# The gate and up products of a decoder layer's FFN by one Strassen step

## The chip, the cores and the metric

One NeuronCore of a Trainium2 chip runs the whole kernel. The metric is the device time of one execution in microseconds (us). TensorE (PE in the profile) multiplies, VectorE (DVE), ScalarE (ACT) and GpSimd (POOL) do the elementwise work, and SyncE (SP), ScalarE and GpSimd issue the transfers. The inputs and the output are float32.

## The reference

One decoder layer on 512 tokens of width 1024: an input projection, sixteen attention heads, a state-space branch, two gated projections that are merged into `w_out`, a layer norm, and a gated feed-forward network (FFN) of hidden width 2816 with a second layer norm. The change lies in the last part:

```
x = layer_norm(DEEPNORM_ALPHA * x + mixed, ln1_g, ln1_b)
h = (silu(x @ w_ffn_gate) * (x @ w_ffn_up)) @ w_ffn_down
x = layer_norm(DEEPNORM_ALPHA * x + h, ln2_g, ln2_b)
```

`x` is 512 by 1024, the gate and up weights are 1024 by 2816, the down weights 2816 by 1024.

## The kernel before

**Products in three parts.** Every float32 operand is split into a high part (a cast to float32r on ScalarE, line 65) and a low part (source minus high part, on VectorE, line 66). A product is three matmuls, high by high, high by low, low by high (`mm3`, lines 97 to 100). Each matmul contracts 128 rows, and each has its own weight load (PEld).

**Weights.** `load_w` (line 85) fetches 128 x 1024 float32 (512 KB) on SP's queue into one of 4 `raw` buffers and splits it into one of 3 `whi` and 3 `wlo` buffers. The split is marked as high priority. The scheduler of the Tile framework writes a fixed order of instructions for each engine from the program order and these priorities, and each engine keeps to its order.

**The output projection, `w_out`** (lines 629 to 692). Its 8 weight chunks come in two halves of 512 columns. Six are loaded and split ahead, the last two of half 0 during the second pair of token tiles (`wo_chunk`, line 638). Tokens go in two rounds `th_` of two tiles of 128: matmuls, `evac_res` (lines 668 to 671, residual and statistics), `layer_norm` (lines 673 to 683), then `transpose_in` (line 165) turns each tile by eight PE transposes and splits it into `x1T`.

**FFN gate and up** (`ffn_pair`, line 709). The hidden width goes in 11 pairs of 128 columns. For each pair the gate product is accumulated over 8 blocks of 128 in PSUM (`gps` banks), then the up product (`cps` banks). Tokens are 512 matmul columns wide, except in the first pair, which does tokens 0 to 255 first and then 256 to 511, so that it can start before the second round is normed. ScalarE takes the tanh of the gate (line 715), VectorE multiplies (lines 716 and 719), and the product `h` is split at once into 22 pairs of 128 x 512 tiles.

**FFN down** (`gemm_down`, line 135) takes the 22 blocks of `h` as stationary operand in two halves of 512 output columns; the last 4 chunks of the second half (`tail`) are done tile by tile of tokens, so that each tile is normed and stored while the next is multiplied.

Of the kernel before, what the change touches and what calls it, by code (L numbers as in the profile page):

```python
# [9 lines left out]
F32 = mybir.dt.float32  # L10
F32R = mybir.dt.float32r
# [26 lines left out]
def tile_hybrid_decoder_layer(  # L38
# [32 lines left out]
    def cps():  # L71
# [13 lines left out]
    def load_w(src, a, b, dst=None):  # L85

        raw = stream.tile([P, 1024], F32, name="raw", bufs=4)
        nc.sync.dma_start(out=raw.rearrange("p (a b) -> p a b", a=a), in_=src.rearrange("(a p) c -> p a c", p=P))
        if dst is None:
            dst = ([stream.tile([P, 1024], F32R, name="whi")], [stream.tile([P, 1024], F32R, name="wlo")])  # L90
# [6 lines left out]
    def mm3(o, l, r, start, stop):  # L97
        nc.tensor.matmul(out=o, lhsT=l[0], rhs=r[0], start=start, stop=False)  # L98
        nc.tensor.matmul(out=o, lhsT=l[0], rhs=r[1], start=False, stop=False)  # L99
        nc.tensor.matmul(out=o, lhsT=l[1], rhs=r[0], start=False, stop=stop)  # L100

# [210 lines left out]
    def group_u(g, ys, gz):  # L312
        uh, ul = big("uh", 4, F32R), big("ul", 4, F32R)
        for c in range(NT):
            cs = slice(c * P, (c + 1) * P)
            y = ys[c]
            nc.vector.scalar_tensor_tensor(out=y, in0=y, scalar=0.5, in1=gz[:, c, :], op0=ALU.mult, op1=ALU.mult)
            ss = sb.tile([P, 2], F32, name="ss")
# [61 lines left out]
    def att_head(h, qk, vt, of):  # L380
# [4 lines left out]
        for i in range(NT):  # L385
            n = (i + 1) * P
            qs = slice(i * P, (i + 1) * P)
            ps = cps()
            nc.tensor.matmul(out=ps[:, 0:n], lhsT=q1[:, qs], rhs=k1[:, 0:n], start=True, stop=False)  # L389
            nc.tensor.matmul(out=ps[:, 0:n], lhsT=q2[:, qs], rhs=k2[:, 0:n], start=False, stop=True)  # L390
            sm = sb.tile([P, 3], F32, name="sm", bufs=6)
# [60 lines left out]

    wraw = stream.tile([P, 1024], F32, name="raw", bufs=4).rearrange("p (a b) -> p a b", a=KD)
    nc.gpsimd.memset(wraw, 0.0)
# [33 lines left out]

    wfh = stream.tile([P, 1024], F32R, name="whi").rearrange("p (a b) -> p a b", a=KD)
    wfl = stream.tile([P, 1024], F32R, name="wlo").rearrange("p (a b) -> p a b", a=KD)  # L490
    split(wfh, wfl, wraw)
# [146 lines left out]
    def wo_chunk(kc, half, dst=None):  # L638
        if (kc, half) not in wo:
            wo[(kc, half)] = down_chunk(w_o, kc, half)  # L640
        return wo[(kc, half)]

    for pair in range(4):
        def evac_a(b, ps):
# [10 lines left out]
    def load_gb(gv, bv):  # L655
        t = slot("gz", (P, 2, D))
# [9 lines left out]
    st6 = [sb.tile([P, 2, 6], F32, name=f"st6{tt}", bufs=1) for tt in range(NT)]  # L666

# [5 lines left out]
    def layer_norm(tt, gb, parts=1):  # L673
        mv = sb.tile([P, 4], F32, name="mv", bufs=4)
        nc.vector.bn_aggr(out=mv[:, 0:2], in_=st6[tt])
# [21 lines left out]
    hslots = []  # L697
    for tag in ("xtok", "xtok", "uh", "ul"):
        b_ = big(tag, 4, F32R)
        hslots += [b_[:, i, :] for i in range(4)]  # L700
    for tag in QK[0] + QK[1] + ("y", "y", "hn"):
        hslots += [slot(tag, (P, T), F32R) for _ in range(2)]
    hT = [(hslots[2 * i], hslots[2 * i + 1]) for i in range(NH - 3)]
    FT = ("dx", "yo", "xw", "sq")

    def ffn_chunks(j2, dst=None):
        return [[ws_chunk(w, j2 * 256, half, dst if w is w_fu and half == 1 else None) for half in range(2)] for w in (w_fg, w_fu)]

    def ffn_pair(j2, s_, chunks=(None, None)):
        n = s_.stop - s_.start  # L710
        t = {}

        def evac_fg(b, ps):
            t[b] = slot(FT[b + 2 * (j2 % 2)])[:, 0:n]
            nc.scalar.activation(out=t[b], in_=ps, func=AF.Tanh, scale=0.5)
            nc.vector.scalar_tensor_tensor(out=t[b], in0=t[b], scalar=1.0, in1=ps, op0=ALU.add, op1=ALU.mult)

        def evac_fu(b, ps):
            nc.vector.scalar_tensor_tensor(out=t[b], in0=t[b], scalar=0.5, in1=ps, op0=ALU.mult, op1=ALU.mult)
            hi, lo = hT[2 * j2 + b]  # L720
            split(hi[:, s_], lo[:, s_], t[b])
        gemm_ws(w_fg, j2 * 256, KD, lambda kt: cols(x1T, kt, s_), evac_fg, gps, n, chunks[0])
        gemm_ws(w_fu, j2 * 256, KD, lambda kt: cols(x1T, kt, s_), evac_fu, cps, n, chunks[1])

    t = [slot("ab", (P, T), F32R) for _ in range(4)]
    chunks = ffn_chunks(0, (t[0:2], t[2:4]))
    ffn_pair(0, slice(0, 256), chunks)
    ffn_pair(0, slice(256, T), chunks)
    hT += [(slot("ab", (P, T), F32R), slot("ab", (P, T), F32R)) for i in range(3)]
    for j2 in range(1, NH // 2):  # L730
        ffn_pair(j2, slice(0, T))

    gb = load_gb(ln2_g, ln2_b)

# [13 lines left out]
    t = [slot(tag, (P, T), F32R) for tag in FT]  # L748
# [31 lines left out]
```

## Time and profile before

| | us |
|---|---|
| three runs | 1166.93, 1169.84, 1170.02 |
| median | 1169.84 |
| profiled execution, its own time | 1168.29 |
| its span, first to last instruction | 1166.6 |
| PE busy in the span | 1140.0 (98%) |
| VectorE busy | 680.6 (58%) |
| ScalarE busy | 468.9 (40%) |
| GpSimd busy | 102.8 (9%) |

The profile shows one execution. A matmul's shown duration includes its way through the array, so the rate is read from the distance between starts. A row "from <- releaser" names the instruction whose end let an idle engine go on. Times are in us from the span's start.

### The profile page before, as it was taken

To read this page: it belongs to the slowest core of one execution; us is meant where nothing else is said; L and a number is where in the kernel's file an instruction comes from. 1 tells how busy PE (TensorE), PEld (TensorE's weight loads), DVE (VectorE), ACT (ScalarE), POOL (GpSimd) and SP (SyncE) were. 2 spreads that over 40 slices of the span, in tenths; PEclk is the share of its full clock that TensorE was granted. 3 is DMA by queue.
4 is the path that set the end of the run, shared out by engine and by line. 5 is a ranking of instruction groups with operands and counts; after the bars stand their busy time and mean duration, and the time that the engine had idled before them with its cause. 6 is when DMAs were issued, how large, how long until landed. Compare 5 with 4: busy or idle time off the path is not lost.

```text
span 1166.6 us, 14040 instructions
## 1 busy us (share of the span) xinstructions
PE 1140.0 (98%) x5390; PEld 926.4 (79%) x5390; DVE 680.6 (58%) x1118; ACT 468.9 (40%) x834; POOL 102.8 (9%) x137
## 2 busy tenths in 40 slices
PE   6999999999999999999999999999999999999997
PEld 5887877778777788777777888889888888888885
DVE  3579964883885664897788345555433433432326
ACT  3376763453441423665566353202323223222120
POOL 2003131030231100210110000010000000000001
PEclk8999999999999999999999999999999999999999
DMA  7343242233221233121212355601333233232221
GB/s 237 98 130 126 74 127 90 77 115 98 91 92 56 89 92 107 39 72 55 73 55 56 91 163 161 196 21 56 107 97 102 91 104 95 91 107 92 91 72 72
DMA packets 93427, 112.58 MB, mean 97 GB/s; under 512 B 4820, under 2 KB 72624, under 8 KB 93232
## 3 DMA queue, kind: packets, MB, share of 16 engines
q1 hardware_dynamic: 90880, 107.03, 29.6%
q10 hardware_dynamic: 1152, 4.19, 1.1%
q0 software_dynamic: 1328, 0.46, 0.3%
q8 instruction: 42, 0.69, 0.2%
q14 instruction: 25, 0.20, 0.1%
HBM read 109.38 MB, written 2.16 MB: 96 GB/s over the span
## 4 chain that ended last, share of the span: by engine, by line
PE 51%; DVE 2%; ACT 0%; issue 0%; POOL 0%; DVEq 0%; ACTq 0%
PE gps L100 11%; PE gps L98 11%; PE gps L99 11%; PE cps L98 5%; PE cps L100 5%; PE cps L99 5%; PE cps L411 1%; PE cps L417 1%; DVE t_sd L682 0%; PE cps L389 0%; PE cps L390 0%; DVE t_sd L670 0%; DVE st L671 0%; PE cps L171 0%; POOL mv L677 0%
## 5 line engine op out<-in xcount | busy, mean ns | idle before, releaser
L66 DVE TENSOR_TENSOR wlo<-raw,whi 128x1024 fp32r<-128x1024 f32 x171 | 210.1, 1229 | 336.7 <-ACT whi L65 336.4
L65 ACT CAST whi<-raw 128x1024 fp32r<-128x1024 f32 x171 | 179.8, 1051 | 418.8 <-PE gps L99 133.5
L98 PE MATMUL gps<-xh,whi 128*128 128x512 f32 (+1 forms) x648 | 252.4, 390 | 0.0
L99 PE MATMUL gps<-xl,whi 128*128 128x512 f32 (+1 forms) x648 | 252.4, 389 | 0.0
L100 PE MATMUL gps<-xh,wlo 128*128 128x512 f32 (+1 forms) x648 | 252.2, 389 | 0.0
L98 PEld LDWEIGHTS gps<-xh,whi 128*128 128x128 f32 x648 | 122.1, 188 | 22.6 <-issue 0.2
L99 PEld LDWEIGHTS gps<-xl,whi 128*128 128x128 f32 x648 | 122.2, 189 | 22.4 <-issue 0.2
L100 PEld LDWEIGHTS gps<-xh,wlo 128*128 128x128 f32 x648 | 122.1, 188 | 21.6
L98 PE MATMUL gps<-whi,xh 128*128 128x512 f32 x208 | 82.7, 398 | 4.4 <-ACT xh L65 4.4
L100 PE MATMUL gps<-whi,xl 128*128 128x512 f32 x208 | 82.4, 396 | 0.0
L99 PE MATMUL gps<-wlo,xh 128*128 128x512 f32 x208 | 82.3, 396 | 0.0
L98 PE MATMUL cps<-xh,whi 128*128 128x512 f32 (+1 forms) x176 | 66.9, 380 | 0.0
L100 PE MATMUL cps<-xh,wlo 128*128 128x512 f32 (+1 forms) x176 | 66.8, 379 | 0.0
L99 PE MATMUL cps<-xl,whi 128*128 128x512 f32 (+1 forms) x176 | 66.8, 379 | 0.0
L677 POOL TENSOR_TENSOR mv<-mv,neghalf 128x1 f32<-128x1 f32 x8 | 9.5, 1192 | 558.6 <-DVE mv L676 558.6
L196 DVE SCALAR_TENSOR_TENSOR t_v<-gps,cw,t_v 128x511 f32<-128x511 f32 (+2 forms) x72 | 53.5, 745 | 3.9 <-ACT t_v L193 3.1
L100 PE MATMUL gps<-t_uh,wlo 128*128 128x512 f32 x128 | 51.0, 399 | 0.0
L99 PE MATMUL gps<-t_ul,whi 128*128 128x512 f32 x128 | 51.0, 398 | 0.0
L98 PE MATMUL gps<-t_uh,whi 128*128 128x512 f32 x128 | 50.5, 395 | 0.0
L98 PEld LDWEIGHTS gps<-whi,xh 128*128 128x128 f32 x208 | 39.7, 191 | 13.6 <-ACT xh L65 5.0
L99 PEld LDWEIGHTS gps<-wlo,xh 128*128 128x128 f32 x208 | 39.7, 191 | 8.6 <-DVE wlo L66 0.5
L100 PEld LDWEIGHTS gps<-whi,xl 128*128 128x128 f32 x208 | 39.6, 190 | 8.4 <-DVE xl L66 0.3
(548 smaller groups left out, 1913.1 us busy)
## 6 DMA issues: line engine op xcount, KB each, us to landing
raw<-in_w_in_dram SPq DMA_DIRECT2D x80, 512.0 KB, 3.7
raw<-in_w_ffn_gate_dram SPq DMA_DIRECT2D x22, 512.0 KB, 3.6
raw<-in_w_ffn_up_dram SPq DMA_DIRECT2D x22, 512.0 KB, 3.6
raw<-in_w_ffn_down_dram SPq DMA_DIRECT2D x22, 512.0 KB, 3.5
t_ab<-ac_d SPq DMA_DIRECT2D x32, 256.0 KB, 3.3
raw<-in_w_proj_ssm_dram SPq DMA_DIRECT2D x16, 512.0 KB, 3.4
raw<-in_w_out_dram SPq DMA_DIRECT2D x8, 512.0 KB, 4.0
raw<-in_w_proj_attn_dram SPq DMA_DIRECT2D x8, 512.0 KB, 4.1
```

The costliest lines, as they stand in the source:

```text
L65: nc.scalar.copy(out=hi, in_=src)
L66: nc.vector.tensor_tensor(out=lo, in0=src, in1=hi.bitcast(F32), op=ALU.subtract)
L98: nc.tensor.matmul(out=o, lhsT=l[0], rhs=r[0], start=start, stop=False)
L99: nc.tensor.matmul(out=o, lhsT=l[0], rhs=r[1], start=False, stop=False)
L100: nc.tensor.matmul(out=o, lhsT=l[1], rhs=r[0], start=False, stop=stop)
L196: nc.vector.scalar_tensor_tensor(out=v[:, sh:], in0=ps[:, 0:T - sh], scalar=cw[:, k, blk:blk + 1], in1=v[:, sh:], op0=ALU.mult, op1=ALU.add)
L411: nc.tensor.transpose(out=ps[:, o:o + P], in_=pr[i][:, kb * P:(kb + 1) * P], identity=ident)
L417: nc.tensor.matmul(out=po[:, kb * P:], lhsT=vt[:, kb, hh, :], rhs=pT[kb][j], start=kb == 0 and j == 0, stop=kb == NT - 1 and j == 1)
L677: nc.gpsimd.tensor_tensor(out=mv[:, 2:3], in0=mv[:, 2:3], in1=neghalf[:, 0:1], op=ALU.pow)
```

## The change

The hidden width goes in 5 blocks of 512 and one of 256. A block's gate product, and its up product, is a 2 by 2 by 2 problem: the block's columns, the 512 tokens and the 1024 contracted rows are each halved. Instead of eight products of quarters there are seven, on sums and differences of quarters, each with 256 tokens as matmul columns.

**Token operands.** Seven operands: two plain quarters (B11, B21) of tokens 0 to 255, split when the first round of tokens is turned; five others (NT1, NT2, T3, T4, B22), made by VectorE (`x_operands`) from a float32 copy `xf` of both rounds, once, and split. All blocks use them.

**Weight operands.** For each gemm seven fetches: a11, a12, a22 plain; s1 and s3 are each a plain fetch on SP's queue and a second, accumulating transfer on GpSimd's queue. VectorE makes the other two sums. All seven are split (`op`, high priority) into four rotating pairs of buffers (`wop0`, `wop1`).

**Sums of products.** Passes with the same bank X, Y or Z accumulate there; ScalarE copies three intermediate states to SBUF (`keep`), VectorE adds (`add`), and the four quadrants then go through the same tanh and multiplications as before.

**Other edits.** `h` is kept in float32 and split at the start of the down phase. The normed tokens go to DRAM on GpSimd's queue and come back for the second residual on ScalarE's queue. All 8 `w_out` chunks are split ahead; the last two follow the attention projection. The last stage's `tail` is 3 chunks and not 4. Buffers are in pools on two sides of SBUF, and a tile waits only for the older tiles under it.

```diff
+    for kc in range(2, 4):
+        t = [slot(tag, (P, T), F32R) for tag in QK[kc - 2]]
+        wo[(kc, 0)] = down_chunk(w_o, kc, 0, (t[0:2], t[2:4]))
...
         for tt in tts:
             for _ in layer_norm(tt, gb):
                 pass
-            transpose_in(x1T, xr[tt], tt)
+            nc.gpsimd.dma_start(out=x1_d[tt], in_=xr[tt])
+            for i in range(2):
+                ps = cps()
+                for k in range(4):
+                    kt = 4 * i + k
+                    nc.tensor.transpose(out=ps[:, k * P:(k + 1) * P], in_=xr[tt][:, kt * P:(kt + 1) * P], identity=ident)
+                ps = ps.rearrange("p (k t) -> p k t", k=4)
+                ts = slice(tt * P, (tt + 1) * P)
+                if th_ == 0:
+                    hi, lo = xop[("B11", "B21")[i]]
+                    split(hi[:, :, ts], lo[:, :, ts], ps)
+                nc.scalar.copy(out=xf[i][:, :, ts], in_=ps)
...
+        nt1 = t_tile().rearrange("p (k t) -> p k t", k=4)
+        v.tensor_tensor(out=nt1, in0=B[1, 1], in1=B[1, 2], op=ALU.subtract)
+        nt2 = new("NT2", lambda t: v.scalar_tensor_tensor(out=t, in0=nt1, scalar=-1.0, in1=B[2, 2], op0=ALU.mult, op1=ALU.subtract))
+        xop["NT1"] = operand(top, "nt1")
+        split(*xop["NT1"], nt1)
+        new("T3", lambda t: v.tensor_tensor(out=t, in0=B[2, 2], in1=B[1, 2], op=ALU.subtract))
+        xop["B22"] = operand(top, "b22")
+        split(*xop["B22"], B[2, 2])
+        new("T4", lambda t: v.scalar_tensor_tensor(out=t, in0=nt2, scalar=-1.0, in1=B[2, 1], op0=ALU.mult, op1=ALU.subtract))
...
+        def load(*src):
+            t = tile_()
+            nc.sync.dma_start(out=v(t), in_=src[0])
+            for s_ in src[1:]:
+                nc.gpsimd.dma_start(out=v(t), in_=s_, accum_op=ALU.add)
+            return t
+
+        def op(t):
+            p_ = wops[nops[0] // 2 % 2]
+            nops[0] += 1
+            o = [p_.tile([P, 1024], F32R, name="w" + i, bufs=2)[:, 0:4 * F] for i in "hl"]
+            with tc.high_priority():
+                split(*o, t)
+            return [v(i) for i in o]
+
+        a11, a12 = load(q(1, 1)), load(q(1, 2))
+        s1 = load(q(2, 1), q(2, 2))
+        s3 = load(q(2, 1), q(1, 1))
+        a22 = load(q(2, 2))
+        yield op(a11)
+        yield op(a12)
+        with tc.high_priority():
+            nc.vector.tensor_tensor(out=a11, in0=s1, in1=a11, op=ALU.add)
+        yield op(a11)
+        yield op(s1)
+        yield op(s3)
+        with tc.high_priority():
+            nc.vector.tensor_tensor(out=a12, in0=a11, in1=a12, op=ALU.add)
+        yield op(a12)
+        yield op(a22)
+
+    PASSES = (("X", "B11"), ("Y", "B21"), ("X", "NT2"), ("Z", "NT1"), ("X", "T3"), ("Z", "B22"), ("X", "T4"))
...
+        for i, (b, x_) in enumerate(PASSES):
...
+            hi, lo = next(ops)
+            xo = xop[x_]
+            for j in range(nj):
+                js = slice(j * P, (j + 1) * P)
+                for k in range(4):
+                    mm3(ps[:, j * 256:(j + 1) * 256], (hi[:, k, js], lo[:, k, js]), (xo[0][:, k, :], xo[1][:, k, :]),
+                        first and j == 0 and k == 0, j == nj - 1 and k == 3, True)
+            if i == 0:
+                keep("a", ps)
+            elif i == 1:
+                quadrant(0, 0, add("a", ps), 1.0)
+            elif i == 2:
+                keep("b", ps)
+            elif i == 3:
+                keep("d", ps)
+            elif i == 4:
+                quadrant(1, 1, add("d", ps), -1.0)
+            elif i == 5:
+                quadrant(0, 1, add("b", ps), 1.0)
+            else:
+                quadrant(1, 0, ps, -1.0)
+            yield
...
+    for b in range(6):
+        gate, up = ffn_block(b)
+        if b == 0:
+            for gen in (gate, up):
+                for _ in range(2):
+                    next(gen)
+            x_operands()
+        for gen in (gate, up):
+            for _ in gen:
+                pass
...
+    for k2 in range(2):
+        h_split(0, k2, t_tile(F32R), t_tile(F32R))
...
+    for b in range(1, 6):
+        for k2 in range(2 if b < 5 else 1):
+            h_split(b, k2, *[htp.tile([P, 1024], F32R, name=f"ht{b}{k2}{i}") for i in "hl"])
...
-    gemm_down(wd_chunk, NH, lhs_h, range(NT), 1, evac_last, lambda: banks.pop(0), 4, (t[0:2], t[2:4]))
+    gemm_down(wd_chunk, NH, lhs_h, range(NT), 1, evac_last, lambda: banks.pop(0), 3)
```

## Rows read from the trace of the kernel before

**Rows 1.** The page: busy time by engine, and the chain that ended last, by engine
```profile
PE 1140.0 (98%) x5390; PEld 926.4 (79%) x5390; DVE 680.6 (58%) x1118; ACT 468.9 (40%) x834; POOL 102.8 (9%) x137
...
PE 51%; DVE 2%; ACT 0%; issue 0%; POOL 0%; DVEq 0%; ACTq 0%
```

**Rows 2.** Timeline of PE, 512-column matmuls: first and last of 57 (start, duration)
```profile
779.84 0.40 PE L99 MATMUL gps<-wlo,xh 128*128 128x512 f32 x1
...
792.55 0.39 PE L98 MATMUL gps<-t_ul,xh 128*128 128x512 f32 x1
```

**Rows 3.** Timeline of PE, 256-column matmuls: first and last of 57
```profile
811.74 0.28 PE L98 MATMUL gps<-xh,whi 128*128 128x256 f32 x1
...
818.46 0.28 PE L100 MATMUL cps<-xh,wlo 128*128 128x256 f32 x1
```

**Rows 4.** Timeline of PE: first 512-column matmul of gate, first of down
```profile
821.46 0.40 PE L98 MATMUL gps<-xh,whi 128*128 128x512 f32 x1
...
1039.09 0.39 PE L98 MATMUL cps<-whi,t_xtok 128*128 128x512 f32 x1
```

**Rows 5.** The chain after the output projection (start, us, what)
```profile
793.85 0.24 PE gps L100
794.11 0.70 DVE t_sd L670
...
796.16 1.20 DVE xl L66 x2
...
800.62 1.29 DVE t_sd L682
...
802.05 1.06 PE cps L171 x8
803.15 1.09 PE cps L171 x8
```

**Rows 6.** VectorE by line, 849 to 1029 (count, busy us, mean ns, idle before)
```profile
L66 DVE TENSOR_TENSOR wlo<-raw,whi 128x1024 fp32r<-128x1024 f32 x33 | 40.4, 1225 | 81.3 <-ACT whi L65 81.3
L716 DVE SCALAR_TENSOR_TENSOR t_dx<-t_dx,gps 128x512 f32<-128x512 f32 x5 | 3.4, 688 | 6.1 <-ACT t_dx L715 6.1
```

**Rows 7.** ScalarE by line, 849 to 1029
```profile
L65 ACT CAST whi<-raw 128x1024 fp32r<-128x1024 f32 x34 | 35.8, 1053 | 92.6 <-PE cps L99 40.3 <-issue 34.8 <-PE gps L99 17.5
L715 ACT ACTIVATE t_dx<-gps 128x512 f32<-128x512 f32 x5 | 3.0, 598 | 9.2 <-PE gps L100 9.2
```

**Rows 8.** Stretches: length; PE, PEld, DVE, ACT, POOL busy (instructions); clock, DMA, GB/s
```profile
849.00:1029.00 180.00, 180.00 (x796) 149.10 (x795) 72.77 (x82) 53.69 (x67) 0.00 (x0) 1.00 0.31 97
1039.00:1099.00 60.00, 60.00 (x267) 49.69 (x266) 17.75 (x18) 12.12 (x12) 0.00 (x0) 1.00 0.29 97
```

**Rows 9.** Timeline of PE at the kernel's start, after a wait of 3.42 us
```profile
15.55 0.80 PE L98 MATMUL gps<-whi,xh 128*128 128x512 f32 x1 [3.42 <-ACT xh L65]
...
19.13 0.63 PE L100 MATMUL gps<-whi,xl 128*128 128x512 f32 x1
19.56 0.63 PE L98 MATMUL gps<-whi,xh 128*128 128x512 f32 x1
...
21.66 0.48 PE L98 MATMUL gps<-whi,xh 128*128 128x512 f32 x1
```

**Rows 10.** DMA issues (count, KB each, median us from issue to landing)
```profile
raw<-in_w_ffn_gate_dram SPq DMA_DIRECT2D x22, 512.0 KB, 3.6
...
raw<-in_w_in_dram POOLq DMA_DIRECT2D x1, 128.0 KB, 6.7
```

**Rows 11.** Timeline of GpSimd: issue of the transfer of 128 KB
```profile
9.41 0.93 POOL L455 DMA_DIRECT2D raw<-in_w_in_dram  x1
```

**Rows 12.** Timeline of VectorE, the last but one tile of tokens
```profile
1153.65 0.69 DVE L670 SCALAR_TENSOR_TENSOR t_sd<-t_sd,gps 128x512 f32<-128x512 f32 x1 [0.99 <-PE gps L100]
...
1156.74 1.41 DVE L682 SCALAR_TENSOR_TENSOR t_sd<-t_sd,mv,t_gz 128x512 f32<-128x512 f32 x2
```

**Rows 13.** Timeline of VectorE: last low part made for the output projection
```profile
753.50 0.69 DVE L651 SCALAR_TENSOR_TENSOR xl<-t_y,xh 128x512 fp32r<-128x512 f32 x1
```

More of the change, by code (lines that the diff above doesn't have):

```diff
@@ L665, in tile_hybrid_decoder_layer @@
         xr.append(t)
-    st6 = [sb.tile([P, 2, 6], F32, name=f"st6{tt}", bufs=1) for tt in range(NT)]
+    st6 = [cst0.tile([P, 2, 6], F32, name=f"st6{tt}") for tt in range(NT)]
     def evac_res(half, tt, ps):
@@ L673, in layer_norm @@
     def layer_norm(tt, gb, parts=1):
-        mv = sb.tile([P, 4], F32, name="mv", bufs=4)
+        mv = cst0.tile([P, 4], F32, name="mv", bufs=4)
         nc.vector.bn_aggr(out=mv[:, 0:2], in_=st6[tt])
@@ L683, in layer_norm, with h_tile, operand @@
             yield s_
-    gb = load_gb(ln1_g, ln1_b)
-    x1T = new_act()
+    gb = load_gb(slot("gz", (P, 2, D)), ln1_g, ln1_b)
+    x1_d = dram.tile([NT, P, D], F32, name="x1_d")
+    right1.close()
+    right2, left2 = ExitStack(), ExitStack()
+    ha = pool(ctx, "ha", "right")
+    bop = pool(right2, "bop", "right")
+    rqp = pool(right2, "rqp", "right")
+    wops = [pool(right2, "wop0", "right")]
+    def h_tile(b):
+        return (hb if b < 4 else ha).tile([P, 4 * T], F32, name="h" if b < 4 else "xf", bufs=4 if b < 4 else 2)
+    xf = [h_tile(4).rearrange("p (k t) -> p k t", k=4) for _ in range(2)]
+    def operand(p_, nm):
+        return [p_.tile([P, 4, 256], F32R, name=nm + i) for i in "hl"]
+    xop = {"B11": operand(bop, "b11"), "B21": operand(bop, "b21")}
     for th_ in range(2):
@@ L693, in tile_hybrid_decoder_layer @@
                 pass
-            transpose_in(x1T, xr[tt], tt)
[L697 to L723, printed above, removed]
@@ new lines, in tile_hybrid_decoder_layer, with t_tile, x_operands, new @@
+    left1.close()
+    hb = pool(ctx, "hb", "left")
+    tp = pool(ctx, "tp", "left")
+    top = pool(left2, "top", "left")
+    wops.append(pool(left2, "wop1", "left"))
+    nops = [0]
+    tmp2 = pool(left2, "tmp2", "left")
+    def t_tile(dtype=F32):
+        return tp.tile([P, 1024], dtype, name="T", bufs=4)
+    def x_operands():
+        B = {(k, t): xf[k - 1][:, :, (t - 1) * 256:t * 256] for k in (1, 2) for t in (1, 2)}
+        def new(nm, make):
+            t = t_tile().rearrange("p (k t) -> p k t", k=4)
+            make(t)
+            xop[nm] = operand(top, nm.lower())
+            split(*xop[nm], t)
+            return t
+        v = nc.vector
+        nt1 = t_tile().rearrange("p (k t) -> p k t", k=4)
[7 more added lines that the diff above has]
+        new("T4", lambda t: v.scalar_tensor_tensor(out=t, in0=nt2, scalar=-1.0, in1=B[2, 1], op0=ALU.mult, op1=ALU.subtract))
@@ new lines, in tile_hybrid_decoder_layer, with ffn_gemm, keep, add @@
+    PASSES = (("X", "B11"), ("Y", "B21"), ("X", "NT2"), ("Z", "NT1"), ("X", "T3"), ("Z", "B22"), ("X", "T4"))
+    def ffn_gemm(w, c0, F, alloc, quadrant):
+        nj = F // P
+        n = nj * 256
+        ops = quarters(w, c0, F)
+        bank = {}
+        cp = {}
+        def keep(nm, src):
+            cp[nm] = tmp2.tile([P, T], F32, name="cp", bufs=4)[:, 0:n]
+            nc.scalar.copy(out=cp[nm], in_=src)
+        def add(nm, src):
+            nc.vector.tensor_tensor(out=cp[nm], in0=src, in1=cp[nm], op=ALU.add)
+            return cp[nm]
+        for i, (b, x_) in enumerate(PASSES):
+            first = b not in bank
+            if first:
+                bank[b] = alloc()[:, 0:n]
+            ps = bank[b]
+            hi, lo = next(ops)
[20 more added lines that the diff above has]
+            yield
@@ new lines, in tile_hybrid_decoder_layer, with ffn_block, gate, up @@
+    hs = []
+    def ffn_block(b):
+        F = 256 if b < 5 else 128
+        nj = F // P
+        n = nj * 256
+        g = {}
+        h = h_tile(b)[:, 0:4 * n]
+        hv = h.rearrange("p (f j t) -> p f j t", f=2, j=nj)
+        hs.append(h)
+        def gate(f, t, o, s):
+            g[f, t] = tmp2.tile([P, T], F32, name="g", bufs=5)[:, 0:n]
+            nc.scalar.activation(out=g[f, t], in_=o, func=AF.Tanh, scale=0.5 * s)
+            nc.vector.scalar_tensor_tensor(out=g[f, t], in0=g[f, t], scalar=1.0, in1=o, op0=ALU.add, op1=ALU.mult)
+        def up(f, t, o, s):
+            nc.vector.scalar_tensor_tensor(out=hv[:, f, :, t * 256:(t + 1) * 256],
+                                           in0=g[f, t].rearrange("p (j t) -> p j t", j=nj), scalar=0.5,
+                                           in1=o.rearrange("p (j t) -> p j t", j=nj), op0=ALU.mult, op1=ALU.mult)
+        return ffn_gemm(w_fg, b * 512, F, gps, gate), ffn_gemm(w_fu, b * 512, F, cps, up)
@@ new lines, in tile_hybrid_decoder_layer, with h_split @@
+    for b in range(6):
[8 more added lines that the diff above has]
+                pass
+    hT = []
+    def h_split(b, k2, hi, lo):
+        split(hi, lo, hs[b][:, k2 * 1024:(k2 + 1) * 1024])
+        for k in range(2):
+            hT.append((hi[:, k * T:(k + 1) * T], lo[:, k * T:(k + 1) * T]))
+    for k2 in range(2):
+        h_split(0, k2, t_tile(F32R), t_tile(F32R))
@@ new lines, in tile_hybrid_decoder_layer @@
+    right2.close()
+    left2.close()
+    wst3 = pool(ctx, "wst3", "right")
+    stream.update({"raw": (wst3, 4), "whi": (wst3, 3), "wlo": (wst3, 3)})
+    end = pool(ctx, "end", "right")
+    htp = pool(ctx, "htp", "left")
+    xr = [end.tile([P, D], F32, name=f"xr{tt}") for tt in range(NT)]
+    for tt in range(NT):
+        nc.scalar.dma_start(out=xr[tt], in_=x1_d[tt])
+    gb = load_gb(end.tile([P, 2, D], F32, name="gb2"), ln2_g, ln2_b)
+    for b in range(1, 6):
+        for k2 in range(2 if b < 5 else 1):
+            h_split(b, k2, *[htp.tile([P, 1024], F32R, name=f"ht{b}{k2}{i}") for i in "hl"])
```

72 lines of the change are left out of this document (40 added, 32 removed).

## The prediction

> **What bounds the kernel now.** I read the page first: PE is busy for 98% of the span, and of the chain that ended last PE holds 51% by the page's count, VectorE 2% [rows 1]. The rest of that chain has no releaser named, but with PE busy throughout there is no room for another engine. So only fewer, or faster, PE instructions can gain, as long as the others keep up. The second view is PE's timeline, read by distance between starts. Of 57 matmuls with 512 columns the first and last are 12.71 us apart, 0.2270 us each [rows 2]. The kernel also has matmuls with 256 columns, in the first pair of the FFN: 6.72 us over 56 distances, 0.1200 us each [rows 3]. That is the form that the whole FFN gets, so its price need not be guessed. Third, the stretches: in 849 to 1029, inside gate and up, PE is busy all the time at full clock (1.00), VectorE 72.8 of 180 us, ScalarE 53.7, the transfers run at 97 GB/s [rows 8].
>
> **PE's work.** Before, gate and up are 22 column blocks x 2 x 8 x 3 = 1056 matmuls of 512 columns, of which the first 96 are done as 192 of 256. From the first 512-column matmul of the second pair to the first of down is 1039.09 - 821.46 = 217.63 us for 960, 0.2267 each [rows 4], so PE doesn't wait there at all. With 192 x 0.120 = 23.04 that makes 240.7 us. After, a gemm of a full block is 7 passes of 2 x 4 x 3 = 24 matmuls with 256 columns; ten such gemms and two of half size are 1848, x 0.120 = 221.8 us. **Gain: 18.9 us.** It isn't an eighth of 240.7 (30.1), because two half matmuls cost 0.240 against 0.2267 [rows 2, 3]. The weight load is no extra bound: it is shown with 0.188 us (149.1 over 795 [rows 8]), yet 256-column matmuls with a load each follow at 0.120 [rows 3]. The Trainium skill (TensorE: Matmul & The Clock Gate, section Back-to-back issue gap) gives columns / 2.4 GHz + 2.5 ns; as an estimate that is 215.8 and 109.2 ns, and a gain of 26.3 us. This trace is 11 ns slower per matmul in both forms, so I keep 18.9.
>
> **VectorE and ScalarE in the steady state.** A full gemm takes PE 168 x 0.120 = 20.2 us. VectorE then has 7 low parts and 2 weight sums of 1024 columns at 1.225, and 3 additions and 4 multiplications of 512 at 0.688 [rows 6]: 11.0 + 4.8 = 15.8 us, 79%. ScalarE has 7 casts at 1.053, and 3 copies and (gate) 4 tanh of 512, both taken at 0.6 [rows 7]: 11.6 us, 57%. Four pairs of operand buffers let a split run four passes (11.5 us) ahead. So both fit, but VectorE goes from 40% to 79%, and an addition has to leave its bank within one pass (2.88 us). From nothing to 5 us over twelve gemms; the two of half size have the least room (passes of 1.44 us, VectorE at 90%). I take **+2.0**.
>
> **The start of the FFN.** This is the costly place. Before, from the end of the output projection (794.09) to 821.46 are 27.37 us: 23.04 of matmuls, 2.15 of transposes, **2.2 of waiting** [rows 4, 5]. After, PE has four passes that need only the first round's tokens, 4 x 2.88 = 11.5, and 2.15 of transposes: 13.7 us of cover. The fifth pass needs NT2, which comes at the end of a chain on VectorE. From 794.1 the residual, statistics and norm of the last two tiles take 803.1 - 794.1 less the two xl of 1.28, some 7.7 us [rows 5]. Ahead of them go the high-priority splits whose buffers PE has just freed, four in that time, 4 x 1.225 = 4.9. Then the transposes (1.1), a copy on ScalarE with its waits (1.1), and nt1, nt2, a cast and a low part, 1.23 + 1.28 + 1.05 + 1.23 = 4.8 (the norm's pass of 1024 took 1.29 [rows 5]). Sum 0.3 + 7.7 + 4.9 + 1.1 + 1.1 + 4.8 = 19.9 us, against 13.7: PE waits 6.2. VectorE then owes NT1, T3, B22, T4 (7.4 us) and the next splits and evacuations (some 6) within four passes (11.5), so T3 or T4 is late by another 1.2. Without the 2.2 of before this is **+5.2**, from 2 (splits not put ahead) to 9 (evacuations ahead of it too).
>
> **The clock.** No row shows PE waiting that long at full clock. At the start of the kernel, after a wait of 3.42 us, matmuls of 512 columns follow each other at 0.43 us, the lower of the two levels (1.2 and 2.4 GHz), until about 21.66 [rows 9]: 6.1 us at half rate, some 3 us lost. From 0 to 3; **+1.5**, half. The Trainium skill (TensorE: Matmul & The Clock Gate, section What's actually happening) has it that an idle TensorE falls to half rate and gets its clock back by activity. By that alone it would be the full 3, and the sum 1.5 us longer; no run here shows it.
>
> **The transfers.** Gate and up fetch seven quarters where they fetched four, 7 x 512 KB in 20.2 us, about 180 GB/s against 97 [rows 8]; a plain one lands in 3.6 us [rows 10] and has a gemm's time. The accumulating transfer isn't in this trace. Lower bound 3.6, like a plain one; upper bound by the GpSimd transfer of 128 KB in 6.7 [rows 10], four times as much, 27 us. There are two per gemm, so with one after the other they bind only above 10.1 us each; I take 5 to 8, nearer the plain row, whose bytes it moves: **0**. Issuing one costs GpSimd under 1 us [rows 11], and its queue has nothing else in the FFN; an accumulation queued behind the wait for its plain half delays only the next one. The buffers come free some eight passes (23 us) before the operand is due.
>
> **Moved steps.** The split of h leaves the FFN and becomes 11 casts and 11 low parts of 1024 in the down phase, where VectorE is busy 17.75 of 60 us [rows 8]: hidden, except for the turn from FFN to down, where the first down chunk must be split into buffers just left by the last gemm: 0 to 3, **+0.8**. The reload of the tokens stands on ScalarE's queue and waits for those buffers too; casts of h behind it have a chunk's time (5.4 us) each, else they add to this term. The last two chunks of the output projection are split earlier, on VectorE and ScalarE after line 644's work, whose last low part ends at 754.2 [rows 13]: 2.8 us more there, against about 3 us until it is read, **0** (up to 0.5). SP's queue issues these before the FFN's. The copy to DRAM is 4 transfers beside other work.
>
> **The tail.** The last four tiles come every 4.08 us (3 chunks x 6 x 0.2267) and not 5.44. VectorE needs 4.5 us for each (1153.65 to 1158.15 [rows 12]), so it falls behind by 0.42 three times: **+1.3**.
>
> **Sum.** -18.9 + 2.0 + 5.2 + 1.5 + 0.8 + 1.3 = -8.1. The profiled execution took 1168.29, so 1160.2; the median of the runs is 1.55 above it, so **1161.7 us**. A measurement of this kernel can tell about 0.3% (3.5 us) from no change.
>
> **Rivals.**
> - *Everything is hidden*: no wait at the start, no clock loss; -18.9 - 2.2 + 1.3, 1150. For it: the chunks of the first round are ready early. Against: VectorE's 7.7 us of norm after the projection can't move. Chance 0.12.
> - *VectorE becomes the bound of the FFN* (the slower side). Its queue is in order, and a low part waits for ScalarE's cast; before, such waits are 81.3 us over 33, 2.5 each, with nothing else to do [rows 6]. If 0.9 of that stays per low part, a gemm needs 15.8 + 6.3 = 22.1 us, and eleven gemms' worth lose 1.9 each, 21 us: 1161.7 - 2.0 + 21, 1181. It decides from 20.2 - 15.8 = 4.4 us of such waits per gemm on. For it: 79%. Against: evacuations fill the waits. Chance 0.14.
> - *The accumulating transfers bind*: above 10.1 us each, every further us costs 22 (20 of full size, 4 of half). At 15 us, 1160 + 108 = 1268. Against: 27 us is a row of many small pieces at the kernel's busiest moment. Chance 0.07.
> - *Little is left*: the start costs 9, the clock 3, the passes 5 and the turn 3 us (in all 21.3 with the tail): within 3.5 us of before. Chance 0.17.
> - The change not doing what it says needs 1848 matmuls not to be there or not to go at 0.120; the rows leave little of that.
>
> The forecast (1155 to 1166) keeps 0.50. Faster: 0.50 + 0.12. Same: 0.17, and 0.02 of VectorE's case. Slower: 0.19. For 8 in 10 the range goes from the hidden case, 1149, to most of VectorE's, 1181.
>
> **What would show it.** Right: 1848 matmuls of 256 columns 0.120 apart, FFN about 235 us long; one wait of 5 to 8 us for NT2 some 14 us after the output projection, with a dip of the granted clock behind it; VectorE at about 80% in the FFN; under 0.2 us of waits per later gemm; the last tile's evacuation 1.3 us late. Wrong: PE waiting in every gemm for a weight operand (VectorE, or a transfer on GpSimd's queue), accumulations landing after 10 us, or no wait at the start.

## The result and the profile after

The changed kernel takes **1178.49 us** (median of 4 runs, 1177.67 to 1178.70), the kernel before 1169.45 (4 runs beside them): a ratio of **1.0080, 95% interval 1.0063 to 1.0098**. It is slower by 0.8%; the forecast was 1161.7. The profiled execution took 1178.42 with a span of 1176.7, 10.1 us more than the 1166.6 of before.

The page of the changed kernel: busy time by engine, and the chain that ended last.

```profile
PE 1138.1 (97%) x6086; PEld 947.5 (81%) x6086; DVE 770.5 (65%) x1210; ACT 525.6 (45%) x906; POOL 135.6 (12%) x165
...
PE 45%; DVE 3%; issue 3%; DMA 1%; ACT 1%; POOL 1%; SPq 0%; DVEq 0%; POOLq 0%; ACTq 0%
```

Against [rows 1], PE was to be busy for some 19 us less, and is for 1.9 us less. So most of the gain was eaten while PE was working, by slower matmuls and by the lower clock, and the rest of the time was lost while it waited. Where this happened is told by the starts of four matmuls, read from PE's timeline (us from the span's start):

| start of | before | after | stage, after less before |
|---|---|---|---|
| last matmul of the attention projection | 748.74 | 757.01 | +8.3 |
| last of the output projection (w_out) | 795.04 | 808.42 | +5.1 |
| first of down | 1039.09 | 1043.96 | -8.5 (FFN) |
| last of down | 1158.69 | 1167.91 | +4.4 |
| end of span | 1166.6 | 1176.7 | +0.9 |

The FFN did get shorter. What surprises is the first line: 8.3 us are lost before any work that the change rewrote. There the matmuls themselves are slower. PE's timeline, first and last of 262 matmuls of 512 columns that follow each other without a break, in the kernel before:

```profile
401.19 0.47 PE L100 MATMUL gps<-xh,wlo 128*128 128x512 f32 x1
...
460.48 0.39 PE L100 MATMUL gps<-whi,xl 128*128 128x512 f32 x1
```

and the same 262 in the changed kernel, with the first and last of 58 in its w_out stage below them:

```profile
404.88 0.48 PE L116 MATMUL gps<-xh,wlo 128*128 128x512 f32 x1
...
465.86 0.40 PE L116 MATMUL gps<-whi,xl 128*128 128x512 f32 x1
...
770.18 0.39 PE L114 MATMUL gps<-t_th,xh 128*128 128x512 f32 x1
...
783.11 0.39 PE L114 MATMUL gps<-t_btok,xh 128*128 128x512 f32 x1
```

59.29 / 261 = 0.2272 us before, 60.98 / 261 = **0.2336** after, and in w_out 12.93 / 57 = 0.2268, as in [rows 2]. The clock is full in all of these.

The second loss is in the w_out stage. VectorE's timeline of the changed kernel:

```profile
770.15 0.69 DVE L687 BATCH_NORM_STATS2 st<-t_sd 128x6 f32<-128x512 f32 x1
778.39 1.22 DVE L807 TENSOR_TENSOR rq<-rq 128x1024 f32<-128x1024 f32 x1 [7.54 <-DMA rq<-in_w_ffn_gate_dram]
779.65 1.23 DVE L812 TENSOR_TENSOR rq<-rq 128x1024 f32<-128x1024 f32 x1
780.79 0.68 DVE L686 SCALAR_TENSOR_TENSOR t_sd<-t_sd,gps 128x512 f32<-128x512 f32 x1
```

Line 807 is the add of the first gate block, a11 += s1. It waits 7.54 us for the accumulating transfer, and behind it in the same queue stands L686, the residual evacuation of w_out. PE's timeline shows what hangs on that:

```profile
783.11 0.39 PE L114 MATMUL gps<-t_btok,xh 128*128 128x512 f32 x1
786.64 1.94 PE L733 MATMUL cps<-ident,t_sd 128*128 128x128 f32 x8 [3.15 <-DVE mv L692]
...
788.81 0.63 PE L116 MATMUL gps<-t_btok,xl 128*128 128x512 f32 x1
789.24 0.63 PE L114 MATMUL gps<-t_cbm,xh 128*128 128x512 f32 x1
...
792.54 0.39 PE L116 MATMUL gps<-t_th,xl 128*128 128x512 f32 x1
```

The transposes need the layer norm, PE idles 3.15 us for them, and afterwards its matmuls follow at 0.43 us, the lower of the two clock levels, until about 792: 5.8 us at half rate, some 2.9 lost.

The stretches of the changed kernel (length; PE, PEld, DVE, ACT, POOL busy with instructions; granted clock, DMA share, GB/s), from w_out to the steady FFN, then down:

```profile
757.00:811.00 54.00, 50.85 (x230) 42.35 (x229) 27.21 (x40) 7.60 (x12) 8.03 (x8) 0.94 0.56 153
811.00:850.00 39.00, 28.67 (x195) 27.10 (x194) 31.05 (x32) 19.10 (x25) 7.51 (x7) 0.87 0.50 131
...
849.00:1029.00 180.00, 180.00 (x1535) 180.00 (x1534) 137.85 (x153) 91.17 (x114) 23.64 (x19) 1.00 0.73 171
...
1060.00:1100.00 40.00, 40.00 (x173) 32.22 (x172) 14.05 (x12) 10.43 (x11) 0.00 (x0) 1.00 0.31 98
```

The steady FFN has no waits: 1535 matmuls in 180 us, 0.1173 each, even less than the 0.1200 of [rows 3], with VectorE at 77% and ScalarE at 51%. The third loss is between 811 and 850, at the start of the FFN: PE is idle for 10.3 us, and a clock of 0.87 over 39 us means that 10 us of it went by at the lower level. PE was still waiting in 1.2 of them, so the clock costs some 4.5 us. PE's waits there, 805 to 850 (total, times, longest):

```profile
PE gps L114 <- ACT nt2h L80: 3.0, 1, 3.0
PE gps L114 <- ACT nt1h L80: 2.0, 1, 2.0
PE cps L733 <- DVE t_sd L698: 1.9, 2, 1.5
PE cps L116 <- DVE wl L81: 1.8, 2, 0.9
PE cps L114 <- ACT wh L80: 1.5, 1, 1.5
```

And the DMA issues of the FFN (count, KB each, median us to landing):

```profile
rq<-in_w_ffn_gate_dram SPq DMA_DIRECT2D x25, 512.0 KB, 6.1
...
rq<-in_w_ffn_gate_dram POOLq DMA_DIRECT2D x10, 512.0 KB, 6.9
rq<-in_w_ffn_up_dram POOLq DMA_DIRECT2D x10, 512.0 KB, 6.0
```

By the median the accumulating ones (POOLq) land in 6 to 7 us, and the plain ones beside them in 6.1 where [rows 10] had 3.6. The one that VectorE waits for above is slower. GpSimd's timeline has its issue, after eight plain loads that SP issued from 757 to 768 us:

```profile
768.62 2.80 POOL L789 DMA_DIRECT2D rq<-in_w_ffn_gate_dram  x2 [168.77 <-PE gps L116]
```

The releaser that it names is a matmul; the same row of run 11 names the plain half of the transfer. The add goes on at 778.39, so this transfer took 9.8 us from its issue.

### The profile page after: what moved, and what is told of

The parts are those of the page before. It is cut to its first block, busy times and chain, and to the rows that moved or that the text cites. A ratio compares the mean times of both kernels' runs of the same rounds, so it can differ in the third digit from the quotient of the medians.

```text
span 1176.7 us, 15773 instructions
## 1 busy us (share of the span) xinstructions
PE 1138.1 (97%) x6086; PEld 947.5 (81%) x6086; DVE 770.5 (65%) x1210; ACT 525.6 (45%) x906; POOL 135.6 (12%) x165
## 4 chain that ended last, share of the span: by engine, by line
PE 45%; DVE 3%; issue 3%; DMA 1%; ACT 1%; POOL 1%; SPq 0%; DVEq 0%; POOLq 0%; ACTq 0%
PE gps L114 9%; PE gps L116 9%; PE gps L115 9%; PE cps L116 5%; PE cps L115 5%; PE cps L114 5%; DMA rq<-in_w_ffn_up_dram 1%; PE cps L433 1%; PE cps L427 1%; DVE xr L698 0%; DVE wl L81 0%; POOL mv L693 0%; PE cps L405 0%; DVE t_sd L698 0%; DMA t_sd<-in_x_dram 0%
## 5 line engine op out<-in xcount | busy, mean ns | idle before, releaser
L81 DVE TENSOR_TENSOR wlo<-raw,whi 128x1024 fp32r<-128x1024 f32 x127 | 156.2, 1230 | 226.5 <-ACT whi L80 226.2
L80 ACT CAST whi<-raw 128x1024 fp32r<-128x1024 f32 x127 | 132.9, 1047 | 279.4 <-PE gps L116 113.1
L114 PE MATMUL gps<-xh,whi 128*128 128x512 f32 x456 | 183.2, 402 | 0.0
L115 PE MATMUL gps<-xl,whi 128*128 128x512 f32 x456 | 183.0, 401 | 0.0
L116 PE MATMUL gps<-xh,wlo 128*128 128x512 f32 x456 | 182.9, 401 | 0.0
L80 ACT CAST wh<-rq 128x1024 fp32r<-128x1024 f32 (+1 forms) x84 | 81.9, 978 | 123.8 <-PE cps L115 46.6
L81 DVE TENSOR_TENSOR wl<-rq,wh 128x1024 fp32r<-128x1024 f32 (+1 forms) x84 | 94.9, 1133 | 42.3 <-ACT wh L80 42.1
L115 PEld LDWEIGHTS gps<-xl,whi 128*128 128x128 f32 x456 | 86.0, 189 | 18.0 <-issue 0.2
L114 PEld LDWEIGHTS gps<-xh,whi 128*128 128x128 f32 x456 | 85.9, 188 | 18.1 <-issue 0.2
L116 PEld LDWEIGHTS gps<-xh,wlo 128*128 128x128 f32 x456 | 86.0, 189 | 17.2
L114 PEld LDWEIGHTS gps<-whi,xh 128*128 128x128 f32 x192 | 36.6, 191 | 13.6 <-ACT xh L80 4.5
```

What stands on the lines that cost most here:

```text
L80: nc.scalar.copy(out=hi, in_=src)
L81: nc.vector.tensor_tensor(out=lo, in0=src, in1=hi.bitcast(F32), op=ALU.subtract)
```

## The experiments

**What differs before the FFN?** The same matmuls in the same order, but other tile pools. The built programs give each tile's address. In the kernel before, 4284 of the 4288 matmuls with 512 columns have both operands at 64 modulo 128 bytes (the streamed whi at 40256, xh0 at 64832). The changed kernel has pools from both ends of the memory: on the left, xh0 at 114624, still 64 modulo 128; on the right, whi at 147424, 96 modulo 128. In its w_out stage both operands come from the left. So the theory is that a matmul's pace hangs on how its two operands' addresses lie to each other.

Run 1: the kernel before, with its operands moved against the streamed weights.

```diff
     sb = ctx.enter_context(tc.tile_pool(name="sb", bufs=2))
+    xtp.tile([P, 8], F32, name="pad")
...
-    st6 = [sb.tile([P, 2, 6], F32, name=f"st6{tt}", bufs=1) for tt in range(NT)]
+    st6all = sb.tile([P, NT, 2, 6], F32, name="st6", bufs=1)
+    st6 = [st6all[:, tt] for tt in range(NT)]
```

> The kernel before with its operand tiles (pools xtp and sb) moved up by 32 bytes against the streamed weights whi and wlo; nothing else of the work changes (the four st6 tiles become one, to make room). Layout theory (what one matmul costs hangs on how the addresses of its stationary and its moving operand lie to each other): 512-column matmuls outside the w_out stage follow at 0.2333 us instead of 0.2267, the end of the attention projection comes about 8 us later (near 757), w_out keeps 0.2267 since both its operands move, the FFN loses about 7 us and down about 3.5; total near 1188 us (1182 to 1195). Rival (the pitch of the changed kernel came from its schedule, its pools' waits or its DMA): no change, 1167 to 1172 us and 0.2267 throughout.

Measured: 1186.9 us, ratio to before 1.0161 (1.0144 to 1.0178). The stretch of 262 in this run:

```profile
404.17 0.48 PE L101 MATMUL gps<-xh,wlo 128*128 128x512 f32 x1
...
465.14 0.40 PE L101 MATMUL gps<-whi,xl 128*128 128x512 f32 x1
```

60.97 / 261 = 0.2336, the pace of the changed kernel to the last digit, and the last matmul of the attention projection starts at 757.07 against 757.01 there. By the same starts the FFN is 6.1 us longer than before and down 3.3, while w_out, where both operands moved together, is 0.3 longer. 32 bytes in front of a pool cost the tuned kernel 19 us.

Run 2: the same with 64 bytes (a pad of `[P, 16]`).

> As the run with 32 bytes, but moved by 64 bytes against the streamed weights. Layout theory: the 512-column pitch goes to 0.2333 as well, total near 1188 us (1180 to 1195), and the 256-column matmuls at the head of the FFN, if they follow the pairs seen in the changed kernel, go from 0.1200 to 0.1146 or 0.117. Rival (no effect of addresses): 1167 to 1172 us, 0.2267 and 0.1200.

Measured: 1178.11 us (1.0084, 1.0069 to 1.0099). Half a miss: the stretch goes from 404.17 to 464.43, 0.2309 on average. Sorted by which operand is stationary (means over distances under 0.3 us), 512 columns take 0.2334 where the moved tile is the stationary one (1107 of them) and only 0.2295 where it is the moving one (2688). The 256-column ones did get faster, 0.1155 as the mean of 142.

Run 3: the other way round, the changed kernel with its operands brought back in line.

```diff
+    pool(ctx, "padr", "right").tile([P, 8], F32, name="pad")
     sba = pool(right1, "sba", "right")
...
+    pool(ctx, "padl", "left").tile([P, 40], F32, name="pad")
     hb = pool(ctx, "hb", "left")
```

> The changed kernel with two unused pads, 32 bytes ahead of the right-hand pools and 160 bytes ahead of the left-hand pools of the FFN, so that both operands of every matmul lie at the same offset modulo 128 bytes, as in the kernel before; the instructions are the same. Layout theory: attention projection ends near 749 us instead of 757.4 (8.3 us less), down plus tail 3.4 us less, FFN matmuls at 0.1200 instead of 0.1175 on average (1848 of them, 4.6 us more); total near 1171 us (1168 to 1174). Rival (the 8.3 us come from the order of the work or the pools' waits): 1177 to 1180 us.

Measured: **1170.25 us**, 8.2 less than the changed kernel (ratio to before 1.0017, 1.0007 to 1.0028). The kernel before stood at 1167.96 beside this run and at 1169.45 beside the changed kernel, so by the ratios it is 7.4 less. The stretch of 262, and the steady FFN:

```profile
399.73 0.48 PE L117 MATMUL gps<-xh,wlo 128*128 128x512 f32 x1
...
458.99 0.39 PE L117 MATMUL gps<-whi,xl 128*128 128x512 f32 x1
```

```profile
849.00:1029.00 180.00, 180.00 (x1503) 180.00 (x1501) 137.01 (x157) 89.47 (x116) 23.11 (x18) 1.00 0.68 157
```

0.2270 again, and in the FFN 180 / 1503 = 0.1198 where the changed kernel had 0.1173. So the change of pools did two opposite things: 512-column matmuls lost 3%, those 256-column ones whose operands lay apart gained. In the changed kernel 2928 of 3328 matmuls with 512 columns have their operands apart, and 992 of 1912 with 256.

**The add that waits.** Run 4 is the changed kernel with one order changed.

```diff
-        with tc.high_priority():
+        with tc.issue_after(stats[3]) if c0 == 0 and w is w_fg else tc.high_priority():
             nc.vector.tensor_tensor(out=a11, in0=s1, in1=a11, op=ALU.add)
```

(the same for a12; `stats` holds the bn_stats instructions of evac_res).

> The changed kernel with the two VectorE adds of the first gate block (a11+s1 and a12+a11) queued behind the residual evacuations of the first half of w_out instead of ahead of them. Queue theory (the add that waits 7.5 us for the accumulating transfer holds the evacuations behind it, so the layer norm and the transposes come late, TensorE idles 3.5 us and then runs 6.8 us at the half clock): the w_out stage shrinks by 3 to 8 us, total 1170.5 to 1175.5 us, and the half-clock stretch near 785 us is gone. Rival (the stage is long because of the transfers and the POOL issues themselves, or the next wait takes its place): less than 1 us off, 1177.5 us or more.

Measured: **1172.28 us** (1.0031, 1.0018 to 1.0044), 6.2 less than the changed kernel, or 5.7 by the ratios. VectorE's timeline and the stretch of w_out:

```profile
777.78 0.69 DVE L686 SCALAR_TENSOR_TENSOR t_sd<-t_sd,gps 128x512 f32<-128x512 f32 x1 [7.02 <-PE gps L116]
...
781.84 1.17 DVE L807 TENSOR_TENSOR rq<-rq 128x1024 f32<-128x1024 f32 x1
```

```profile
757.00:811.00 54.00, 52.52 (x266) 44.24 (x264) 31.83 (x46) 11.25 (x18) 12.21 (x10) 1.00 0.61 167
```

The evacuation now goes when its matmuls are done, the add finds its data there, and the clock stays at 1.00. From 756.93 to 802.33 the stage takes 45.4 us, against 51.4 in the changed kernel and 46.3 before. The transfers are as many as ever (167 GB/s), so they were not the cost; the place of one instruction in a queue was.

**Both, with an eye on the faster 256-column pace.** Run 5 puts the pads of run 3 and the order of run 4 together, with pads of 64 bytes ahead of pool `top` and 192 ahead of `wop1`.

> The changed kernel with the pads of the aligned run, two more pads so that five of the seven product passes have their stationary and moving operands 64 bytes apart (modulo 128), and the first gate block's adds queued behind the evacuations. If the two causes are separate and add: 1170.3 for the aligned run less 6.2 for the order (1178.5 less 1172.3) less about 2.6 for the offset (those passes at 0.1146 instead of 0.1200, the whole FFN at 0.1161 on average against 0.1175 in the changed kernel), so near 1160 us (1157 to 1163). Rival (both remove the same wait): no better than the aligned run, 1168 us or more.

Measured: 1159.97 us (0.9937, 0.9923 to 0.9952). The total is as expected, but not by its parts: the FFN matmuls came at 0.1185 instead of 0.1161. (Against the 0.1198 of run 3, from which the sum starts, 0.1161 would have been worth some 7 us and not 2.6; 0.1185 is worth 2.4.) Run 10 asks further about that.

**The start of the FFN.** In run 4 VectorE's timeline shows what the sum NT1 (L765) stands behind:

```profile
810.02 1.29 DVE L698 SCALAR_TENSOR_TENSOR t_sd<-t_sd,mv,t_gz 128x1024 f32<-128x1024 f32 x1 [0.46 <-POOL mv L693]
811.22 0.68 DVE L833 TENSOR_TENSOR cp<-gps,cp 128x512 f32<-128x512 f32 x1
811.82 3.48 DVE L81 TENSOR_TENSOR wl<-rq,wh 128x1024 fp32r<-128x1024 f32 x3
815.23 1.22 DVE L807 TENSOR_TENSOR rq<-rq 128x1024 f32<-128x1024 f32 x1
816.36 0.68 DVE L878 SCALAR_TENSOR_TENSOR g<-g,cp 128x512 f32<-128x512 f32 x1
816.96 1.21 DVE L812 TENSOR_TENSOR rq<-rq 128x1024 f32<-128x1024 f32 x1
818.10 1.21 DVE L81 TENSOR_TENSOR wl<-rq,wh 128x1024 fp32r<-128x1024 f32 x1
819.23 1.21 DVE L765 TENSOR_TENSOR T<-xf 128x1024 f32<-128x1024 f32 x1
```

Run 6 is run 5 with one line more, which gives NT1 and what follows from it priority:

```diff
-            x_operands()
+            with tc.high_priority():
+                x_operands()
```

> The run before this one, with the activation sums and splits (NT1, NT2, T3, B22, T4) given high priority, so that VectorE takes them ahead of the next weight blocks' sums and splits. Queue theory (at the start of the FFN VectorE is never idle from 801 to 831 us and the first NT1 subtraction stands at 819.2 behind sums and splits of weights that are needed later): the waits for nt1h and nt2h (5.2 us together) and part of the half-clock stretch go, total 3 to 7 us less than the run before this one. Rival (VectorE has that much to do whatever the order, so that the weights come late instead): within 1 us of the run before this one.

Measured: **1153.49 us** (0.9878, 0.9863 to 0.9892), 6.5 less than run 5. PE's waits from 790 to 840, and the stretch that was at 0.87:

```profile
PE cps L734 <- DVE t_sd L699: 1.9, 2, 1.5
PE gps L116 <- DVE nt2l L82: 1.5, 1, 1.5
PE cps L117 <- DVE wl L82: 1.2, 2, 0.8
PE cps L115 <- ACT wh L81: 0.9, 1, 0.9
```

```profile
811.00:850.00 39.00, 36.94 (x310) 36.75 (x311) 36.59 (x39) 21.54 (x26) 5.12 (x4) 1.00 0.75 181
```

In VectorE's timeline NT1 (line 769 here) now starts 11.8 us after the last matmul of w_out (792.34), and not 16.9 as in run 4:

```profile
804.09 1.22 DVE L769 TENSOR_TENSOR T<-xf 128x1024 f32<-128x1024 f32 x1
```

VectorE is no less busy (36.6 of 39 us); it only does first what PE needs first. The 5 us of waits for nt1h and nt2h have become 1.5 for nt2l, and with short waits the clock stays at 1.00.

Run 7 is run 6 with passes three and four exchanged.

> The same with passes three and four exchanged: the NT1 product is done before the NT2 product, and its weights are split first. Theory: NT2 hangs on NT1 by one VectorE pass, a cast and a subtraction (3.5 us), which 24 matmuls of NT1 (2.8 us) would cover; total another 1 to 3 us less. Rival: the chain is already hidden or the weights come last, no difference over 1 us.

Measured: 1158.64 us (0.9927, 0.9910 to 0.9943), 5.2 *more* than run 6: a miss. PE still waits 1.6 us for nt2l, so the NT1 product in between hid nothing, and a new wait of 1.1 us has come up, for ScalarE's copy out of a bank. That is 1 us more than in run 6 at the start of the FFN. Another 3 us go in stops of up to 0.3 us that recur in every gemm from 837 us on, where the T3 product starts, and that run 6 doesn't have. PE's and ScalarE's timelines at one of them:

```profile
857.64 0.28 PE L115 MATMUL gps<-b22h,wh 128*128 128x256 f32 x1
857.93 0.39 PE L115 MATMUL gps<-t3h,wh 128*128 128x256 f32 x1
...
857.30 0.58 ACT L834 COPY cp<-gps 128x512 f32<-128x512 f32 x1
```

T3's first matmul starts as ScalarE's copy out of a bank ends (857.88). That these copies hold T3 in every gemm is read from such rows; no run tests it. Together that is 4 of the 5.2 us.

**Are the accumulating transfers worth it?** Run 8 is the changed kernel without them.

```diff
-        s1 = load(q(2, 1), q(2, 2))
-        s3 = load(q(2, 1), q(1, 1))
+        s1 = load(q(2, 1))
         a22 = load(q(2, 2))
+        s3 = tile_()
+        nc.gpsimd.memset(s3[:, 0:1], 0.0)
...
+        nc.vector.tensor_tensor(out=s3, in0=s1, in1=a11, op=ALU.add)
         with tc.high_priority():
+            nc.vector.tensor_tensor(out=s1, in0=s1, in1=a22, op=ALU.add)
```

> The changed kernel with no accumulating transfers: the sums s1 and s3 are made by VectorE from the plain loads (two more 128x1024 adds of about 1.22 us per product call, 24 in all, and a third fewer loads of FFN weights, since two of seven go away). Forecast's reading (the accumulating transfers are hidden in steady state, and VectorE has room): steady FFN at the same matmul pitch with VectorE at 87 to 92% instead of 76 to 79%, the w_out stage 2 to 6 us shorter since no add waits for an accumulating transfer; total 1172 to 1177 us. Rival (VectorE becomes the bound of the FFN once it makes the sums): PE waits for weights in every block, 1182 us or more.

The expectation has two of seven loads go away; by the edit it is three, from seven to four per call. Measured: **1167.47 us** (0.9998, 0.9989 to 1.0007), 11 less than the changed kernel (9.6 by the ratios) and 4.5 below the range. The steady FFN:

```profile
849.00:1029.00 180.00, 180.00 (x1535) 179.83 (x1535) 156.93 (x181) 92.06 (x121) 0.89 (x9) 1.00 0.29 89
```

VectorE is at 87%, and PE gets through the same 1535 matmuls. So in the steady state neither way costs anything, and VectorE is not the bound even with two more adds per call. The gain lies ahead of it: w_out takes 45.9 us (756.73 to 802.64; no add has to wait for 7 us), and the FFN 4.4 us less than in run 4, all of it at its start, where fewer sums stand ahead of NT1.

Run 9 and run 10: run 6 with the sums of run 8, and that with other pads.

> The run with the operand chain first, now with the sums s1 and s3 made by VectorE as in the run with vector sums. There the accumulating transfers' removal gave 4.8 us over the run that only queued the adds behind (1172.3 to 1167.5), of which 4.4 lay in the FFN's first 30 us. If that was because fewer weight sums and splits stood ahead of the operand chain, the chain-first order has taken it already: 1151 to 1154 us against 1153.5. Rival (the accumulating transfers themselves slow the start, through the DMA engines or GpSimd's queue): another 3 to 5 us, 1148.5 to 1150.5 us. If VectorE is now too full at the start (87% already in steady state), 1155 us or more.

> The same kernel with other pads: five of seven passes with their stationary operand at 96 and their moving operand at 32 modulo 128 (the pair that ran at 0.1146 in the changed kernel) instead of 64 and 0 (which ran at 0.118). Theory (the pitch hangs on the two offsets themselves, not only on their difference): the FFN's matmuls go from 0.1184 to about 0.116 on average, 4 to 5 us less in the FFN than the run before this one. Rival (only the difference counts, and what differed was the schedule): less than 1 us off.

Measured: 1155.91 us (0.9889, 0.9868 to 0.9909) and 1157.06 (0.9905, 0.9881 to 0.9929). Run 9 misses its 1151 to 1154 and lands where the expectation had VectorE too full. Without the transfers run 6 gets no better, by the medians 2.4 us worse, with intervals that overlap; run 9's trace has a wait of 1.9 us for a cast `wh` at 835.66, where run 6 has none. That it isn't faster speaks for VectorE's order as what run 8 gained at the start of the FFN, since run 6 has mended it already. And the offsets 96 and 32 ran at 0.1179 (mean of 1301), like 64 and 0 in run 6 (0.1178 of 1314), not at the 0.1147 that the same pair had in the changed kernel (654). So the residues modulo 128 don't settle the fast pace of the 256-column matmuls; what else does, stays open.

**What is left of the forecast.** Run 11 is run 3 and run 4 together and nothing else.

> The changed kernel with both unforeseen costs removed and nothing else: all operands at the same offset modulo 128 as in the kernel before (FFN matmuls at 0.1200), and the first gate block's adds queued behind the evacuations. This is what the forecast's sum was made for (1161.7 us). If the two corrections add: 1178.5 less 8.2 less 6.2, 1164 us (1162 to 1166), and what is left against the forecast is the start of the FFN (waits of 12 us where the sum had 7.4 less the 2.2 of before). Rival (the steady state or the end of the kernel also missed the sum): 1167 us or more.

Measured: **1164.97 us** (0.9963, 0.9951 to 0.9975): a little faster than before, as the sum had it, by 3.3 us and not 8.1. By the starts in its trace (749.32, 794.67, 1033.70, 1154.24, end 1163.4) the stages differ from before by -1.0 (w_out), -5.0 (FFN), +0.9 (down) and +1.3 (end); the 0.6 that are left lie ahead of w_out, in work that is the same in both.

## Why the prediction was wrong

**Missing from the sum: the pools.** The forecast costed operations that are removed, added and moved; the new pools it took as free. They made matmuls of 512 columns slower in stages that the change doesn't touch, and it is there that the sign was lost: 7.4 to 8.2 us net (run 3). Ahead of w_out 8.3 were lost; in down run 3 takes 3.5 back (123.95 to 120.47); the FFN, the other way, grows by 3.9 when the pads are put in (235.5 to 239.5). That this was the addresses is shown from both sides (runs 1 and 3).

**The transfers: the step "0".** In the steady state it was right: 6 to 7 us by the median against 5 to 8, never binding. What failed is that it was argued for the steady state alone ("The buffers come free some eight passes (23 us) before the operand is due"). For the first block there are no eight passes: its loads start at the end of the attention projection, its accumulating transfer is issued 11 us later and takes 9.8 us, the add stands in VectorE's queue in the middle of w_out, and holds what is behind it. The sum priced that at nothing; it was 5.7 to 6.2 us (run 4). What is queued behind the waiting instruction was asked of GpSimd's queue, where the answer is harmless, and not of VectorE's. (An issue took GpSimd 1.4 us and not under 1, 2.80 for two; no wait of PE in the steady state comes of it.)

**The start of the FFN: mechanism right, size off.** PE did wait for NT2, after the four passes, with a dip of the clock behind it. Start and clock were to be +5.2 and +1.5, with 2.0 more for VectorE in the steady state; in run 11 the FFN gains 5.0 where PE's work alone gives 18.9, so they are 13.9. The term that was too small is the work ahead of NT1 on VectorE, four splits ("4 x 1.225 = 4.9"): the first NT2 matmul of run 11 starts 23.7 us after the evacuation that the sum counts from, and not 19.9. The rows of run 4 show, between the end of the norm (811.3) and NT1 (819.2), four splits, two weight sums and two evacuation steps, 7.9 us, with one more split ahead of the norm's second half. Run 6 puts the chain ahead of most of these and wins 6.5 us. Nor was it one wait. Of the 10.2 us in the changed kernel's rows, 5.0 are for NT1 and NT2 (forecast 6.2), 1.9 for the last round's transposes, which the forecast did not have, and 3.3 for parts of weights, where it had 1.2 for T3 or T4. The 2.2 of waiting in the kernel before was misread: the last matmul of w_out starts at 795.04, after the 794.09 that was taken for the end, so PE waited 1.0; the forecast's 13.7 us of cover are too short by the same 1.2, and +5.2 stays. The clock's share was 4.5 us in the changed kernel, not 1.5: waits of 2.0 and 3.0 us follow each other, and two more (1.5 and 0.9) soon after bring the lower level back. The Trainium skill (TensorE: Matmul & The Clock Gate, section What's actually happening) has an idle TensorE fall to half rate. The trace agrees with that: the clock fell behind the waits of 2.0 and 3.0 us. In run 6 waits of up to 1.5 us left it at 1.00.

**PE's work: right.** 1848 matmuls at 0.120, when the operands lie as they did before (0.1198 in run 3). The Trainium skill (TensorE: Matmul & The Clock Gate, section Back-to-back issue gap) adds 2.5 ns to columns / 2.4 GHz, as the gap of an isolated matmul. That is not met here: 0.2267 and 0.2336 are 13 and 20 ns above 512 columns at 2.4 GHz, and 256 columns came at 0.1173 to 0.1200, 10.6 to 13.3 ns above.

**VectorE's steady state: wrong side of its range.** 2.0 us were taken and none was lost: no wait of PE from 850 to 1040, VectorE at 77% against 79%. The rival with VectorE as the bound falls; run 8 takes it to 87% without a wait. That rival's 1181 is near the measured time, but for another reason.

**Turn and tail: right.** +0.8 and +1.3 were forecast, +0.9 and +1.3 are left in run 11.

## What to carry to other kernels

When a change moves tiles to other pools, compare the pace of matmuls that it doesn't touch, over a few hundred of them, before looking for any wait: here the place of the pools took 7 to 8 us, more than the 3.3 that the change brings once that and the waiting add are mended. A steady-state argument doesn't cover the first block: follow its transfer to the instruction that waits for it, and read what stands behind that one on its own engine. And an engine that is 77% busy on average can still be late where a stage begins; what helped there was order (6.5 us for one line), not less work.

With all three corrections, and pads that give five of seven passes a faster pace (0.1178), the change does pay: run 6, at 1153.49 us, beats the kernel before by 1.2% and the changed one by 25 us.

## What the runs showed of the hardware

- The distance between matmuls of 512 columns depends on the two operands' addresses: 0.2267 to 0.2272 us with the same residue modulo 128 bytes, 0.2336 with 32 bytes between them (run 1, and the changed kernel), and 0.2295 or 0.2334 with 64, depending on which of the two is the stationary one (run 2).
- With 256 columns it is the other way: 0.1198 to 0.1200 with the same residue, 0.1147 to 0.1179 as means with 64 bytes between. The residues alone don't explain that spread (run 10).
- Accumulating transfers of 512 KB landed in 6 to 7 us by the median, the first one, beside eight plain loads, in 9.8. The plain ones beside them took 6.1 and 4.9 us in the changed kernel, and 3.7 and 3.6 in run 8, which has no accumulating ones and four plain ones per gemm instead of five.
